# Layer-1 experts: wide and narrow experts alternate block by block, in a TensorE order written in the program, with a gather by rows and a combine in two parts

## The chip, the cores and the metric

The kernel runs on one core of one Trainium2 chip. The metric is the device time of one launch in microseconds (us), as the median of several runs. The core has a matrix engine (PE, with its weight loads shown apart as PEld), a vector engine (DVE), a scalar engine (ACT), a general engine (POOL) and SP, whose queue issues almost all of the DMA transfers. PE writes to PSUM, of which the kernel uses 8 banks of 512 fp32 per partition.

## The reference, cut to what matters

A block of two layers on 256 tokens of width 1024 is followed by a second block of two layers. The change lies in the second layer of the first block, in its mixture of 8 experts with a hidden width of 2816. Each token goes to its two best experts:

```
logits = tokens @ router_w                       # 256 x 8
top_vals, top_idx = top_k(logits, 2);  gates = softmax(top_vals)
for each expert e, over its tokens xb:
    y = (silu(xb @ w1[e]) * (xb @ w3[e])) @ w2[e]
out[token] += gate * y
```

All numbers are fp32. The weights of the 8 experts, 8 x 3 x 1024 x 2816 x 4 bytes = 276.8 MB, are read from HBM once.

## The kernel before

`moe` (line 1171) sorts the experts by their token count. Five places take up to 96 tokens and are called wide here (m = 96, `NL = 5`), three take up to 64 and are called narrow (m = 64). The first place always belongs to expert 0. The rest of the tokens, if any, go through a slow path under `tc.If` (line 1373); no instruction of it shows in the trace.

A `Job` is one expert at its place. Its constructor gathers the expert's tokens: a one-hot matrix `oh` (256 tokens x m slots, in two halves) is multiplied with the tokens, which are kept as a high and a low fp32r part `uh`. Line 1199 uses 128 columns of the tokens as the stationary operand and the one-hot as the moving one, so that the product comes out transposed, features on partitions, in `xg`: 8 groups of features x 4 matmuls with m columns, 32 per job. Two transposes of the one-hot (line 1205) make `oht` for the combine.

The hidden width is cut into blocks of 1024, 1024 and 768. A unit is one block of one job, and consists of three steps:

- `up(i)`: 8 transfers of weights (two of w1 and w3 for each pair of feature groups), then matmuls whose stationary operand is 32 columns of `xg` (wide, four of them side by side on PE) or 64 (narrow, two side by side). A wide job has three such waves for each feature group, in three PSUM banks, a narrow one two, in two banks. ACT then applies silu (line 1236) and DVE multiplies (line 1238), giving `h`.
- `turn(i)`: 8 transposes of `h` (6 for the block of 768) through two banks named hT, copied by ACT and DVE (line 1252).
- `down(i)`: 4 (or 3) transfers of w2, and matmuls that add into the output banks `y` for all three blocks: two banks for a wide job, one for a narrow one. For each 128 of the hidden width there are one and a half waves (wide) or one (narrow).

`combine` (line 1277) brings `y` back to the tokens: for each half of the features it splits `y` into a high and a low part (ACT, DVE), multiplies each with `oht` for both halves of the tokens (line 1296, four matmuls), and DVE adds gate times the product into `acc`, shown as macc (line 1300). For a wide job the second half first needs two copies and a sum (lines 1285 to 1287), because its output lies in parts of two banks.

The loop at line 1332 goes over the units, one expert after another, in the order of `PLACES`: wide, narrow, wide, wide, narrow, wide, wide, narrow. For unit u it calls `up(u)`, then, at the last block, the constructor of the next job, then at the second block the `combine` of the job before, then `down` of the unit before, then `turn(u)`. This is the order of the program; the order on each engine is made by the scheduler of the framework, which may move an instruction that is ready ahead of others. That is how matmuls of a gather or a combine come to stand between those of `up`.

Weights come through `raw` (line 194), which rotates over a ring of SBUF buffers of 1 MB each and issues the transfer on SP's queue as soon as the buffer's last reader is done. The expert's number is loaded into a register on SP (`values_load`, line 1328) ahead of its weights.

The pool of PSUM banks of this stage is set at line 1951: 3 for `up` (tag g), 2 for `y`, 3 (tag b) for all the rest: xg, ohT, hT, comb. Before the stage, PE does a piece of a later layer (`last_v`, shown as lv); after it comes the first layer of the second block, whose first weights are loaded ahead by `prime`.

The later layers' own experts, in `block2`, have a gather of another form (lines 1678 to 1695): the one-hot is the stationary operand and 512 columns of tokens are the moving one, so that rows of tokens come out, in `xs`; eight transposes make `xg` of them.

Of the kernel before, what the change touches and what calls it, by code (L numbers as in the profile page):

```python
# [11 lines left out]
F32 = mybir.dt.float32  # L12
F32R = mybir.dt.float32r
# [9 lines left out]
KC = D // 128  # L23
# [13 lines left out]
CONV = "pvpvpvpp"  # L37
KEX = 4
CAPS = (64,) * KEX + (128,) + (64,) * 5 + (32,) * 6
NL, PLACES = 5, (0, 5, 1, 2, 6, 3, 4, 7)  # L40


def layout(widths):
# [112 lines left out]
class Net:  # L156
# [1014 lines left out]
    def moe(self, E, F, uh, oh0, rank, slot, gates, w1, w3, w2, acc, mp):  # L1171


        nc, tc = self.nc, self.tc
# [3 lines left out]
        def onehot(sl, m, base=0):  # L1178
            oh = mp.tile([128, 2, 96], F32R, tag="oh", name="oh", bufs=2)
            b = base % 128  # L1180
            nc.vector.tensor_tensor(oh[:, :, :m], iotas[base // 128][:, None, b:b + m].to_broadcast([128, 2, m]),
                                    sl[:, :, None].to_broadcast([128, 2, m]), OP.is_equal)
            return oh
# [3 lines left out]
        class Job:  # L1187

            def __init__(j, ws, oh, m, gcol, first):
                j.w = [w.rearrange("(k p) n -> p k n", p=128) for w in ws[:2]]  # L1190
                j.w2, j.m, j.gcol, j.first = ws[2], m, gcol, first
                j.y, j.h, j.hT = None, {}, {}
                j.xg = xg = mp.tile([128, KC, 96], F32, tag="xg", name="xg", bufs=2)
                for k0 in (0, 4):
                    p = self.bank("xg")
                    for i in range(4):
                        o = p[:, i * m:(i + 1) * m]
                        for q in range(4):
                            nc.tensor.matmul(o, uh[q // 2][:, q % 2, (k0 + i) * 128:(k0 + i + 1) * 128], oh[:, q % 2, :m],
                                             start=(q == 0), stop=(q == 3))  # L1200
                    (nc.vector.tensor_copy if k0 else nc.scalar.copy)(xg[:, k0:k0 + 4, :m],
                                                                     p[:, :4 * m].rearrange("p (k t) -> p k t", k=4))
                p = self.bank("ohT")
                for tt in range(2):
                    nc.tensor.transpose(p[:m, tt * 128:(tt + 1) * 128], oh[:, tt, :m].bitcast(F32), self.ident)
                j.oht = mp.tile([128, 256], F32R, tag="oht", name="oht", bufs=2)
                nc.scalar.activation(j.oht[:m], p[:m, :256], AF.Copy)

            def up(j, i):
# [64 lines left out]
                                             start=(i == 0 and k == (k % 2 if b else 0)), stop=(i == len(blocks) - 1 and k >= nk - 2),  # L1274
                                             tile_position=(0, c * t), skip_group_check=True)

            def combine(j):
                m, y = j.m, j.y
                for o in range(2):
                    js = slice(o * 512, (o + 1) * 512)  # L1280
                    src = y[0][:m]
                    if o:
                        if m == 96:
                            src = mp.tile([128, 512], F32, tag="ysum", name="ysum")[:m]
                            nc.scalar.copy(src[:64], y[1][64:128])
                            nc.scalar.copy(src[64:96], y[0][96:128])
                            nc.vector.tensor_tensor(src[:64], y[1][:64], src[:64], OP.add)
                        else:
                            src = y[0][64:128]
                    yg = [self.wkp.tile([128, 512], F32R, tag="room", name="y" + c, bufs=2) for c in "hl"]  # L1290
                    nc.scalar.activation(yg[0][:m], src, AF.Copy)
                    nc.vector.tensor_tensor(yg[1][:m], src, yg[0][:m].bitcast(F32), OP.subtract)
                    for tt in range(2):
                        p = self.bank("comb")
                        for hl in range(2):
                            nc.tensor.matmul(p, j.oht[:m, tt * 128:(tt + 1) * 128], yg[hl][:m], start=(hl == 0), stop=(hl == 1))
                        if j.first:
                            nc.vector.tensor_scalar(acc[:, tt, js], p, j.gcol(tt), None, op0=OP.mult)
                        else:
                            nc.vector.scalar_tensor_tensor(acc[:, tt, js], p, j.gcol(tt), acc[:, tt, js],  # L1300
                                                           op0=OP.mult, op1=OP.add)

        nb = len(blocks)
# [21 lines left out]
        def job(q):  # L1325
            if q == 0:
                return first
            e = nc.values_load(idx[0:1, q:q + 1], engines=(mybir.EngineType.SP,), min_val=0, max_val=E - 1)
            m = 96 if q < NL else 64
            return Job((w1[e], w3[e], w2[e]), onehot(W[:, 0:2, q], m), m, lambda tt: W[:, 2 + tt, q:q + 1], False)  # L1330

        units = [(q, i) for q in PLACES for i in range(nb)]
        jobs = {}
        behind = None
        for u, (q, i) in enumerate(units):
            if u == 0:
                jobs[q] = job(q)
            jobs[q].up(i)
            if i == nb - 1 and u + 1 < len(units):
                q2 = units[u + 1][0]  # L1340
                jobs[q2] = job(q2)
            if i == 1 and behind is not None:
                jobs.pop(behind).combine()
                behind = None
            if u:
                q1, i1 = units[u - 1]
                jobs[q1].down(i1)
                if i1 == nb - 1:
                    behind = q1
            jobs[q].turn(i)  # L1350
        q, i = units[-1]
        jobs[q].down(i)
        jobs.pop(q).combine()


        capv = mp.tile([128, E], F32, name="capv")
# [16 lines left out]
        with self.aside(), tc.If(cnt > self.OV):  # L1373
            rp = mp.tile([128, 2, E], F32, name="rp")
            nc.vector.tensor_tensor(rp, slot, capv[:, None, :].to_broadcast([128, 2, E]), OP.subtract)
            with tc.For_i(0, E, 1) as ei:
                nc.vector.tensor_scalar(ecur, ecur, 1.0, None, op0=OP.add)
                sel = mp.tile([128, E], F32, name="osel")
                nc.vector.tensor_scalar(sel, eid, ecur, None, op0=OP.is_equal)
                pc = mp.tile([128, 2, 2], F32, name="opc")  # L1380
                junk = mp.tile([128, E], F32, name="ojunk")
                for tt in range(2):
                    for i, src in enumerate((rp, G)):
                        nc.vector.scalar_tensor_tensor(junk, src[:, tt, :], 1.0, sel, op0=OP.mult, op1=OP.mult,
                                                       accum_out=pc[:, tt, i:i + 1])
                for b in range(3):
                    j = Job((w1[ei], w3[ei], w2[ei]), onehot(pc[:, :, 0], 64, 64 * b), 64, lambda tt: pc[:, tt, 1:2], False)
                    for i in range(nb):
                        j.up(i)
                        j.turn(i)  # L1390
                        j.down(i)
                    j.combine()
# [509 lines left out]
    def run(self):  # L1902
        nc, t, tc = self.nc, self.t, self.tc
        part = self.part
        with ExitStack() as es:
# [42 lines left out]
                if "l1" in part:  # L1948
                    gpf = self.conv1(mrow)
            e0.close()  # L1950
            self.banks = {"g": 3, "y": 2, "b": 3}
            self.psp = e0.enter_context(tc.tile_pool(name="ps2", bufs=1, space=PSUM))
            if "l1" in part:
                self.moe_layer1(gpf)
# [7 lines left out]
            o = self.out[0].rearrange("(t p) d -> p t d", p=128)  # L1962
# [32 lines left out]
```

## Time and profile before

| what | us |
|---|---|
| median of 3 runs | 2187.96 |
| lowest, highest | 2182.73, 2188.52 |
| the profiled execution | 2188.77 |
| its span, first to last instruction | 2186.9 |
| stage of the layer-1 experts, first `up` to last `down` | 764.6 to 1489.2 |

The trace holds one execution. Times in it count from the first instruction. A row of the timeline is a group of equal instructions: start, length, engine, line, operation, what it writes and reads, partitions x columns, count, and in brackets the engine's idle time before and who ended it. An fp32 matmul of the source shows as two instructions. A matmul's bar holds its latency, and bars of matmuls that run side by side overlap. `128*32 128x512` is a stationary operand of 128 partitions by 32 columns and a moving one of 512 columns. In a window's row the columns behind the busy times are the granted clock of PE as a share of full speed, the mean busy share of the 16 DMA engines, and GB/s.

### The profile page before, as it was taken

Reading aid. Unit: us, or ns where it says so; the run is one execution under the profiler, and the core shown is the slowest. Engines: PE = TensorE matmul, PEld = TensorE weight load, DVE = VectorE, ACT = ScalarE, POOL = GpSimd, SP = SyncE. Lnnn points to the kernel's source line nnn. Section 1 sums busy time; section 2 is a strip of 40 time slices with the busy share of each in tenths; the row PEclk is TensorE's granted clock in tenths of the full one; section 3 lists DMA queues with packets and bytes.
Section 4 is the critical chain, followed back from the end, with each engine's and each line's share of the span. In section 5 each row is a group of like instructions: output and inputs, shape, how many; then the busy total and the mean of one; then the engine's idle time right before and its main releaser. Section 6 shows DMA issues by size and latency. Waiting matters only on the chain. (4 is left out here: it accounts for less than half of the span.)

```text
span 2186.9 us, 32516 instructions
## 1 busy us (share of the span) xinstructions
PE 2022.2 (92%) x13393; PEld 1129.1 (52%) x13393; DVE 827.8 (38%) x1695; ACT 573.6 (26%) x965; POOL 84.4 (4%) x121
## 2 busy tenths in 40 slices
PE   6999897999889899999999999998989987989996
PEld 2777666889867533433344333345733424943331
DVE  4465466444887400111101101015642315662223
ACT  3453345334534300100101001014422212532210
POOL 1010100000120000000000000002000001000000
PEclk9999998999999999999999999998989999999998
DMA  7532547873622689999899998997389999489995
GB/s 289 189 124 93 203 165 274 271 268 116 208 88 99 231 338 374 411 393 361 319 374 402 410 361 315 361 408 278 123 358 386 394 390 365 145 314 404 375 387 245
DMA packets 166338, 634.56 MB, mean 290 GB/s; under 512 B 11952, under 2 KB 53040, under 8 KB 124192
## 3 DMA queue, kind: packets, MB, share of 16 engines
q1 hardware_dynamic: 163808, 630.76, 76.1%
q8 instruction: 111, 1.82, 0.3%
q0 software_dynamic: 2080, 1.04, 0.2%
q10 hardware_dynamic: 288, 0.52, 0.1%
q14 instruction: 51, 0.42, 0.1%
HBM read 631.20 MB, written 1.05 MB: 289 GB/s over the span
## 5 line engine op out<-in xcount | busy, mean ns | idle before, releaser
L1226 PE MATMUL up<-raw,xg 128*32 128x512 f32 (+3 forms) x3456 | 437.6, 559 | 0.1
L256 DVE TENSOR_TENSOR wh<-raw,wh 128x1024 fp32r<-128x1024 f32 x182 | 222.6, 1229 | 178.9 <-ACT wh L255 177.7
L1226 PEld LDWEIGHTS up<-raw,xg 128*32 128x32 f32 (+1 forms) x3456 | 147.4, 114 | 250.8 <-issue 238.4
L255 ACT ACTIVATE wh<-raw 128x1024 fp32r<-128x1024 f32 x182 | 190.7, 1058 | 230.5 <-PE gT L192 88.9
L1272 PE MATMUL y<-raw,hT 128*32 128x512 f32 (+1 forms) x1584 | 218.1, 604 | 0.0
L1728 PE MATMUL up<-raw,xg 128*64 128x512 f32 (+1 forms) x1088 | 205.0, 594 | 4.8 <-DMA raw<-in_w_up 2.9
L1238 DVE TENSOR_TENSOR h<-up,h 64x512 f32<-64x512 f32 (+5 forms) x63 | 40.8, 648 | 389.1 <-ACT h L1236 388.3
L1236 ACT ACTIVATE h<-up 64x512 f32<-64x512 f32 (+5 forms) x63 | 35.0, 555 | 430.7 <-PE up L1226 430.5
L1754 PE MATMUL y<-raw,hT 128*64 128x512 f32 (+1 forms) x576 | 133.2, 597 | 9.0 <-DMA raw<-in_w_down 4.4
L1728 PEld LDWEIGHTS up<-raw,xg 128*64 128x64 f32 (+1 forms) x1088 | 62.8, 127 | 130.9 <-issue 120.9
L1272 PEld LDWEIGHTS y<-raw,hT 128*32 128x32 f32 (+1 forms) x1584 | 60.6, 116 | 123.8 <-issue 116.4
L190 PE MATMUL gT<-fuTh,wh 128*128 128x256 f32 x352 | 101.0, 287 | 0.0
L1734 DVE TENSOR_TENSOR h<-up,h 64x512 f32<-64x512 f32 x28 | 29.6, 1056 | 188.6 <-ACT h L1733 188.6
L191 PE MATMUL gT<-fuTl,wh 128*128 128x256 f32 x352 | 99.5, 283 | 0.0
L192 PE MATMUL gT<-fuTh,wh 128*128 128x256 f32 x352 | 99.5, 283 | 0.0
L445 PE MATMUL mod<-raw,cs 128*32 128x512 f32 x384 | 62.9, 692 | 26.0 <-DMA raw<-in_l_mod_w 26.0
L1754 PEld LDWEIGHTS y<-raw,hT 128*64 128x64 f32 (+1 forms) x576 | 38.4, 124 | 94.0 <-issue 64.7
L1733 ACT ACTIVATE h<-up 64x512 f32<-64x512 f32 x28 | 30.0, 1072 | 188.7 <-PE up L1728 188.7
L190 PEld LDWEIGHTS gT<-fuTh,wh 128*128 128x128 f32 x352 | 67.4, 191 | 12.1 <-issue 10.9
L192 PEld LDWEIGHTS gT<-fuTh,wh 128*128 128x128 f32 x352 | 67.5, 192 | 0.4
L191 PEld LDWEIGHTS gT<-fuTl,wh 128*128 128x128 f32 x352 | 67.4, 192 | 0.2
L1252 DVE COPY hT<-hT 128x384 f32<-128x384 f32 (+3 forms) x24 | 10.8, 449 | 120.7 <-PE hT L1251 120.7
(573 smaller groups left out, 3212.8 us busy)
## 6 DMA issues: line engine op xcount, KB each, us to landing
raw<-in_l_moe_w SPq DMA_DIRECT2D x216, 1024.0 KB, 8.9
raw<-in_w_gate SPq DMA_DIRECT2D x64, 1024.0 KB, 8.9
raw<-in_w_up SPq DMA_DIRECT2D x64, 1024.0 KB, 9.1
raw<-in_w_down SPq DMA_DIRECT2D x64, 1024.0 KB, 11.9
raw<-in_l_mod_w SPq DMA_DIRECT2D x48, 1024.0 KB, 6.2
raw<-in_l_moe_w SPq DMA_DIRECT2D x64, 768.0 KB, 6.4
raw<-in_l_ffn_w SPq DMA_DIRECT2D x33, 1024.0 KB, 5.4
raw<-in_l_w_in SPq DMA_DIRECT2D x14, 1024.0 KB, 5.4
```

The costliest lines, as they stand in the source:

```text
L190: mm(out, l[0], r[0], start=start, stop=False, skip_group_check=True)
L191: mm(out, l[0], r[1], start=False, stop=False, skip_group_check=True)
L192: mm(out, l[1], r[0], start=False, stop=stop, skip_group_check=True)
L255: nc.scalar.activation(hi, x[:, k:k + s, :], AF.Copy)
L256: nc.vector.tensor_tensor(lo, x[:, k:k + s, :], hi.bitcast(F32), OP.subtract)
L445: nc.tensor.matmul(p[32 * j:32 * j + 32, :], self.cs[:, k, :], x[:, 0, j * 512:(j + 1) * 512], start=(k == 0), stop=(k == KC - 1), tile_po ...
L1226: nc.tensor.matmul(ps[b][c * t:(c + 1) * t, :hn], j.xg[:, k, s:s + t], x[w][:, k - k2, half * hn:(half + 1) * hn], start=(k == 0), stop=(k ...
L1236: nc.scalar.activation(h[a:z, js], ps[b1][o1:o1 + z - a, :hn], AF.Silu)
L1238: nc.vector.tensor_tensor(h[a:z, js], ps[b3][o3:o3 + z - a, :hn], h[a:z, js], OP.mult)
L1272: nc.tensor.matmul(j.y[b][c * t:(c + 1) * t, :], hT[:, k, s:s + t], x[:, k - k2, o * 512:(o + 1) * 512], start=(i == 0 and k == (k % 2 if ...
L1728: nc.tensor.matmul(p[o:o + t, :], xg[:, k, c:c + t], pair[w][:, k - k4, :], start=(k == 0), stop=(k == KC - 1), tile_position=(0, o))
L1754: nc.tensor.matmul(y[o][a:a + n, :], hT[:, q * m + a:q * m + a + n], x[e][:, k, o * 512:(o + 1) * 512], start=(q == 0), stop=(q == 3), til ...
```

## The change

The units of wide and narrow experts alternate: the first wide expert's three blocks come first, then blocks are drawn from the row of the other 12 wide ones and from the row of the 9 narrow ones, from whichever has the larger share left. So two jobs are open at a time. The order is (place, block) 0.0 0.1 0.2, 1.0 5.0 1.1 5.1 1.2 5.2 2.0, 2.1 6.0 2.2 6.1 3.0 6.2 3.1, 3.2 7.0 4.0 7.1 4.1 7.2 4.2.

The whole loop stands in `manual_schedule` for PE: PE's instructions keep the order of the program. The other engines are scheduled as before.

The constructor now gathers rows: 8 matmuls with the one-hot as the stationary operand and 512 columns moving, into `xs`, copied by ACT and DVE. The new `begin` transposes these (8 transposes) into `xg` and makes `oht`. The constructor stands ahead of the `up` of the unit before the new job's first, `begin` behind that `up`. `combine` is called for one half of the features between `up` and `down`, and for the other behind `down`, ahead of `turn`.

Three buffers in place of two hold `xg` and `oht`, two of a new tag hold `xs` and `ysum`. PSUM: 3 banks for `y` in place of 2, and 2 in place of 3 for all the rest. The slow path calls `begin` as well.

```diff
-NL, PLACES = 5, (0, 5, 1, 2, 6, 3, 4, 7)
+NL = 5
...
-                j.xg = xg = mp.tile([128, KC, 96], F32, tag="xg", name="xg", bufs=2)
+                j.oh = oh
+                j.xs = xs = [mp.tile([128, 512], F32, tag="half", name="xs", bufs=2) for _ in range(2)]
+                for c in range(2):
+                    cs = slice(c * 512, (c + 1) * 512)
+                    p = self.bank("xs")
+                    for q in range(4):
+                        nc.tensor.matmul(p[:m], oh[:, q % 2, :m], uh[q // 2][:, q % 2, cs], start=(q == 0), stop=(q == 3))
+                    (nc.vector.tensor_copy if c else nc.scalar.copy)(xs[c][:m], p[:m])
+
+            def begin(j):
+                m, xs = j.m, j.xs
+                j.xg = xg = mp.tile([128, KC, 96], F32, tag="xg", name="xg", bufs=3)
                 for k0 in (0, 4):
                     p = self.bank("xg")
                     for i in range(4):
-                        o = p[:, i * m:(i + 1) * m]
-                        for q in range(4):
-                            nc.tensor.matmul(o, uh[q // 2][:, q % 2, (k0 + i) * 128:(k0 + i + 1) * 128], oh[:, q % 2, :m],
-                                             start=(q == 0), stop=(q == 3))
+                        nc.tensor.transpose(p[:, i * m:(i + 1) * m], xs[k0 // 4][:m, i * 128:(i + 1) * 128], self.ident[:m, :m])
...
-            def combine(j):
+            def combine(j, halves=(0, 1)):
                 m, y = j.m, j.y
-                for o in range(2):
+                for o in halves:
...
-        units = [(q, i) for q in PLACES for i in range(nb)]
...
+        streams = [[(q, i) for q in qs for i in range(nb)] for qs in (range(NL), range(NL, E))]
+        units, streams[0] = streams[0][:nb], streams[0][nb:]
+        total = [len(x) for x in streams]
+        while any(streams):
+            units.append(streams[max((0, 1), key=lambda x: len(streams[x]) / total[x])].pop(0))
+        with tc.manual_schedule(engines={mybir.EngineType.PE}):
+            jobs = {units[0][0]: job(units[0][0])}
+            jobs[units[0][0]].begin()
+            done = None
+            for u, (q, i) in enumerate(units):
+                new = u + 1 < len(units) and units[u + 1][1] == 0 and units[u + 1][0]
+                if new:
+                    jobs[new] = job(new)
+                jobs[q].up(i)
+                out, done = done, None
+                if out is not None:
+                    jobs[out].combine((0,))
+                if new:
+                    jobs[new].begin()
+                if u:
+                    q1, i1 = units[u - 1]
+                    jobs[q1].down(i1)
+                    if i1 == nb - 1:
+                        done = q1
+                if out is not None:
+                    jobs.pop(out).combine((1,))
+                jobs[q].turn(i)
+            if done is not None:
+                jobs.pop(done).combine()
+            q, i = units[-1]
+            jobs[q].down(i)
+            jobs.pop(q).combine()
...
-            self.banks = {"g": 3, "y": 2, "b": 3}
+            self.banks = {"g": 3, "y": 3, "b": 2}
```

## Rows read from the trace of the kernel before

**Rows 1.** The page, part 1: busy time of the engines, share, count.

```profile
PE 2022.2 (92%) x13393; PEld 1129.1 (52%) x13393; DVE 827.8 (38%) x1695; ACT 573.6 (26%) x965; POOL 84.4 (4%) x121
```

**Rows 2.** Windows (experts' stage, then three short ones): busy of each engine.

```profile
core 0: us, PE busy (x) PEld busy (x) DVE busy (x) ACT busy (x) POOL busy (x), PEclk, DMA share, GB/s
764.60:1489.20 724.60, 718.23 (x5511) 268.33 (x5510) 90.08 (x148) 65.83 (x126) 0.00 (x0) 0.99 0.96 371
840.00:860.00 20.00, 20.00 (x133) 6.24 (x134) 0.85 (x3) 0.85 (x2) 0.00 (x0) 0.88 0.94 351
1200.00:1220.00 20.00, 18.83 (x124) 6.56 (x124) 1.41 (x3) 1.34 (x3) 0.00 (x0) 0.91 1.02 415
1660.00:1680.00 20.00, 18.39 (x92) 8.65 (x90) 7.95 (x12) 6.00 (x8) 0.00 (x0) 1.00 0.98 385
```

**Rows 3.** Waits of the experts' stage: who waited for whom, us, times, longest.

```profile
PEld up L1226 <- DMA raw<-in_l_moe_w: 2.3, 8, 0.4
...
SPq L200 <- PE up L1226: 363.7, 148, 7.2
SPq L200 <- PE y L1272: 178.7, 78, 9.5
```

**Rows 4.** Groups by line, same stage: count, busy us, mean ns, idle before.

```profile
L1226 PE MATMUL up<-raw,xg 128*32 128x512 f32 (+3 forms) x3456 | 437.6, 559 | 0.1
...
L1272 PE MATMUL y<-raw,hT 128*32 128x512 f32 (+1 forms) x1584 | 218.1, 604 | 0.0
...
L1238 DVE TENSOR_TENSOR h<-up,h 64x512 f32<-64x512 f32 (+5 forms) x63 | 40.8, 648 | 389.1 <-ACT h L1236 388.3
...
L1300 DVE SCALAR_TENSOR_TENSOR macc<-comb,W,macc 128x512 f32<-128x512 f32 x24 | 17.5, 749 | 53.1 <-PE comb L1296 53.1
...
L1252 ACT COPY hT<-hT 128x384 f32<-128x384 f32 (+1 forms) x24 | 10.5, 439 | 119.9 <-PE hT L1251 119.9
```

**Rows 5.** Timeline of PE, two stretches of blocks: start, length, matmuls, count.

```profile
827.70 7.60 PE L1226 MATMUL up<-raw,xg 128*32 128x384 f32 x92
835.23 0.41 PE L1199 MATMUL xg<-oh,muhh 128*128 128x64 f32 x2
...
1211.77 20.83 PE L1226 MATMUL up<-raw,xg 128*32 128x512 f32 x192
1232.53 1.94 PE L1272 MATMUL y<-raw,hT 128*64 128x512 f32 x8
```

**Rows 6.** Timeline of PE: a run of transposes, then runs of a combine.

```profile
867.75 7.93 PE L1272 MATMUL y<-raw,hT 128*32 128x512 f32 x72
875.61 1.09 PE L1251 MATMUL hT<-cst,h 64*128 64x64 f32 x8
876.63 13.95 PE L1226 MATMUL up<-raw,xg 128*64 128x512 f32 x64
...
1064.24 3.63 PE L1226 MATMUL up<-raw,xg 128*32 128x512 f32 x28
1067.80 0.50 PE L1296 MATMUL comb<-yh,oht 96*128 96x512 f32 x1
...
1068.45 2.77 PE L1226 MATMUL up<-raw,xg 128*32 128x512 f32 x20
```

**Rows 7.** Timeline of PE in the later stage: a gather by rows and transposes.

```profile
1674.66 0.63 PE L1685 MATMUL xs<-muhh,oh 128*128 128x512 f32 x2
...
1676.05 0.63 PE L1685 MATMUL xs<-muhl,oh 128*128 128x512 f32 x2
1677.78 1.09 PE L1693 MATMUL xg<-cst,xs 128*128 128x128 f32 x8 [1.11 <-ACT xs L1686]
1678.71 0.38 PE L1703 MATMUL ohT<-cst,oh 128*128 128x128 f32 x2
```

**Rows 8.** Timeline of PE, then DVE: the end of the last expert.

```profile
1476.99 12.24 PE L1272 MATMUL y<-raw,hT 128*64 128x512 f32 x56
...
1494.12 1.41 DVE L1300 SCALAR_TENSOR_TENSOR macc<-comb,W,macc 128x512 f32<-128x512 f32 x2 [0.81 <-PE comb L1296]
```

More of the change, by code (lines that the diff above doesn't have):

```diff
@@ L1204, in __init__ @@
                 for tt in range(2):
-                    nc.tensor.transpose(p[:m, tt * 128:(tt + 1) * 128], oh[:, tt, :m].bitcast(F32), self.ident)
-                j.oht = mp.tile([128, 256], F32R, tag="oht", name="oht", bufs=2)
+                    nc.tensor.transpose(p[:m, tt * 128:(tt + 1) * 128], j.oh[:, tt, :m].bitcast(F32), self.ident)
+                j.oht = mp.tile([128, 256], F32R, tag="oht", name="oht", bufs=3)
                 nc.scalar.activation(j.oht[:m], p[:m, :256], AF.Copy)
@@ L1283, in combine @@
                         if m == 96:
-                            src = mp.tile([128, 512], F32, tag="ysum", name="ysum")[:m]
+                            src = mp.tile([128, 512], F32, tag="half", name="ysum", bufs=2)[:m]
                             nc.scalar.copy(src[:64], y[1][64:128])
@@ L1330, in job @@
             return Job((w1[e], w3[e], w2[e]), onehot(W[:, 0:2, q], m), m, lambda tt: W[:, 2 + tt, q:q + 1], False)
-        units = [(q, i) for q in PLACES for i in range(nb)]
[L1333 to L1353, printed above, removed]
+        streams = [[(q, i) for q in qs for i in range(nb)] for qs in (range(NL), range(NL, E))]
[30 more added lines that the diff above has]
+            jobs.pop(q).combine()
         capv = mp.tile([128, E], F32, name="capv")
@@ L1387, in moe @@
                     j = Job((w1[ei], w3[ei], w2[ei]), onehot(pc[:, :, 0], 64, 64 * b), 64, lambda tt: pc[:, tt, 1:2], False)
+                    j.begin()
                     for i in range(nb):
```

## The prediction

> **What bounds the kernel now.** I read the page's busy times first, then windows over the stage of the layer-1 experts, the waits inside it, its groups by line, and at last the timeline of PE. PE is busy for 92% of the span [rows 1], and in the experts' stage for 718 of 724.6 us [rows 2]; but a matmul's bar contains its latency, so this does not yet say that PE is the limit. DMA's share is 0.96 in the same stage [rows 2], so either could be it. The waits decide: the weight loads of `up` waited for an expert's weights 2.3 us in all, 0.4 us at the longest, while the queue that issues those weights waited for PE's matmuls to give a buffer back 363.7 + 178.7 us, 226 times of 280 issues [rows 3]. Weights are there before PE wants them; PE's own instruction stream is the bound, and the stage is worth what is taken off that stream.
>
> The stream has a floor. A wave of four 32-column matmuls, or of two 64-column ones, takes 0.43 us for 512 columns: 56 narrow matmuls are 28 waves in 12.24 us, of which the last bar is some 0.6 [rows 8]. With 384 columns it is three quarters, 0.32: 92 matmuls, 23 waves, in 7.5 us [rows 5]. Each fp32 matmul of the source is two of the trace, so the 3456 + 1584 of the stage [rows 4] are, by the plans at `up` and `down`, 162 waves at 512 columns and 48 at 384 for each of five wide experts, 108 and 32 for each of three narrow ones, 1134 and 336 together: 487.6 + 108.4 = 596.0 us. The change touches none of them. The other 724.6 - 596.0 = 128.6 us are gathers, transposes of h, combines, waits and clock, put between the waves in 98 runs, of which [rows 6] shows some. That is the pool from which a gain can come.
>
> **The change, part by part.** A run's price is start of the group before it, plus its waves at 0.43, to the start of the group after it. Eight transposes of h: 867.75 + 18 x 0.43 = 875.49, next group 876.63, so 1.14 [rows 6]; I take 1.2, and 1.1 for the six of a 768-wide block. Two combine matmuls: 1064.24 + 7 x 0.43 = 1067.25, next group 1068.45, so 1.2 [rows 6]. Gathering by rows is done by the later stage already: eight 512-column matmuls from 1674.66 to 1676.51, 0.23 each, and eight transposes with two of the one-hot from 1677.78 to about 1678.93, 1.15 together, behind a wait of 1.11 us for the copy between them [rows 7]. From these, for the stage after:
>
> - Turns. 24 units, one run each, since `down` of the unit before stands ahead of it and gives h time: 16 x 1.2 + 8 x 1.1 = 28.0.
> - Gathers. Seven jobs (the first lies before the stage): 56 matmuls at 0.23 = 12.9, standing right behind a turn, so with no run of their own; and 7 x 1.15 = 8.1 for `begin`. The copy's wait of 1.11 is hidden by a whole `up` of at least 10 us put between the two. They replace 224 matmuls and 14 transposes that today stand in scattered runs.
> - Runs of `begin` and of a combine's first half between `up` and `down`: by the order of units there are 11. The fixed part of a run is 1.14 - 8 x 0.11 = 0.26 at a turn and 1.2 - 2 x 0.23 = 0.74 inside `up` [rows 6]; I take the middle, 0.5: 5.5.
> - Combines: 12 halves of four matmuls at 0.23 = 11.2 before the last two jobs, and expert 7's whole combine ahead of the last `down`, 0.3 + 8 x 0.23 + a wait of 1.1 = 3.3.
> - Alternating widths: `up` of a wide block straight into `down` of a narrow one, or the reverse, 11 times without a run between. The row with such a passage shows 1211.77 + 48 x 0.43 = 1232.41 against 1232.53 [rows 5]: 0.12 each, 1.3 in all. The Trainium skill (TensorEngine Tiling, Key Properties) says that changing the tiling mode drains the engine; taken as the fixed part of a whole run, 0.26 to 0.74, that would be 3 to 8 us and not 1.3. The row shows a far smaller drain between two column tilings, and the row goes into the sum.
> - Waits from having two banks for everything but `up` and `y`, where there were three. PE's order is now fixed, so whatever stands behind a bank's copy waits too. The trace of before does not show this arrangement. Lower end: nothing, as the copies are short and off PE. Upper end by the nearest rows, one DVE or ACT operation late each time: 0.3 per gather for the copy of hT (439 ns [rows 4], mostly beside four transposes); 1.0 per `begin`, whose one-hot transposes need a third bank and whose copy queues on ACT behind the silu of h; 0.7 per second half of a combine (macc takes 749 ns [rows 4], twice); 1.5 at the two places where combine and `begin` meet and macc queues on DVE behind three products of h at 648 ns [rows 4]. That is 2.1 + 7.0 + 4.2 + 3.0 = 16.3. I take the whole, being the end that rows support; none excludes twice that.
> - Clock. Two windows show 0.88 and 0.91 [rows 2], that is (0.12 + 0.09) x 20 = 4.2 us lost to half clock. I keep 4.2.
>
> Sum: 596.0 + 28.0 + 12.9 + 8.1 + 5.5 + 11.2 + 3.3 + 1.3 + 16.3 + 4.2 = 686.8, so 37.8 us less. Two things are not free but small: the first job's gather, which now has a copy in its middle but fewer matmuls, 0 +- 0.5; and the end, where a wide expert is last instead of a narrow one. Today the last matmul of `down` ends at 1489.2 and the last macc at 1495.5 [rows 8]; a wide one adds two copies and a sum of about 0.6 each, partly beside the first half: +1.2. Net 36.6.
>
> Is the cover for this still there? DMA is what comes next: 280 transfers, 276.8 MB. At the 415 GB/s of a full window [rows 2] they take 667 us, 20 under PE's 687, and the first buffers of the ring are filled before the stage begins. The register loads for the expert numbers stand on SP ahead of the weights of a unit, once per job, on values ready since before the stage: nothing. The next stage's first four weight loads still follow the last expert's in the same queue.
>
> The profiled execution took 2188.8 us, 0.8 above the median of the three runs; 2188.8 - 36.6 = 2152.2, and on the median's scale **2151 us**. About 0.3% (6.6 us) is what a measurement of this kernel can tell from no change.
>
> **Rivals.**
> First, DMA takes over. Its share is 0.96 [rows 2]; if that were real occupancy, the stage could not get shorter than 0.96 x 724.6 = 696, a gain of 29 - 1 = 28: 2161. Against it: a full window moves 415 GB/s, the stage's mean is 371 [rows 2], and weights wait for buffers. For it: narrow blocks take PE 22 us for 30 us of weights, so stretches of them eat the lead.
>
> Second, nothing gained: if the bank waits are three times my upper end, 49 us, the gain is 36.6 - 32.6 = 4: 2184, inside the 0.3%. For it: a fixed order lets nothing slip past a wait; against it: today's waits of this kind, which the profile puts at a few us, arise with the same copies.
>
> Third, slower, by the clock. In the window from 1200 us PE did narrow waves at 384 columns and a turn, and the clock fell; in the one from 840 us it was still low behind a run of 34 gather matmuls of 64 columns at 835.23 [rows 2, 5]. The change puts eight more transposes into each job and sets them in runs with the one-hot's, the combine's halves and h's. If every one of the 36 runs after let the clock fall once, at the 0.12 x 20 = 2.4 us that the window from 840 us lost, against the 4.2 us in the sum, it would cost 36 x 2.4 - 4.2 = 82 us: 2233. It decides against the change from 15 such falls on beyond today's (36.6 / 2.4). Against it: the later stage runs the same matmuls and transposes with a wait of 1.1 us in the middle, and its window has a clock of 1.00 [rows 7, 2]. The Trainium skill (TensorE: Matmul & The Clock Gate, Part 4: PE-mode transpose) says that transposes do not count as busy work for the clock, which is the rule that speaks against gathering by transposes. By that rule this rival is right; the window of the later stage does not bear it out for groups of ten between dense matmuls.
>
> **How the numbers follow.** Forecast, waits from none to twice the upper end: the gain runs from 36.6 + 16.3 + 4.2 = 57 down to 36.6 - 16.3 = 20, 2131 to 2168, chance 0.64. DMA: 0.12 (faster too). Waits between two and three times, 2168 to 2181: 0.06. Nothing gained: 0.08. Slower: 0.10, of which the clock has 0.06. So faster 0.82, same 0.08, slower 0.10; the range from 2130 to 2180 leaves out the last two and little else.
>
> **What would show it.** Right: waves unchanged in number and pace; runs of other matmuls down from 98 to about 36; no more gather matmuls with 64 or 96 columns; PE's stage near 687 us; DMA's rate in it near 390 GB/s; waits of `up` for weights still a few us. Wrong step by step: waits of transposes or one-hot transposes for DVE or ACT above 16 us in all (banks); waits of `up` for weights above 10 us (DMA); more than two windows with a clock under 0.95 (clock). A stage time above 718 us would make the forecast wrong.

## The result, and the profile after

| what | before | after |
|---|---|---|
| median (runs taken side by side) | 2186.15 us, 4 runs, 2182.73 to 2188.52 | 2157.77 us, 4 runs, 2149.66 to 2160.15 |
| ratio, 95% interval | | 0.9855, 0.9837 to 0.9873 |
| the profiled execution | 2188.77 us | 2155.77 us |
| its span | 2186.9 us | 2153.9 us |

The change makes the kernel 1.45% faster. The forecast was 2151 us, in a range from 2130 to 2180. Placed on the two profiled executions, the time went here:

| stretch | before | after | difference | forecast |
|---|---|---|---|---|
| start to first `up` | 764.6 | 761.9 | -2.7 | 0 +- 0.5 |
| layer-1 experts' stage | 724.6 | 688.9 | -35.7 | -37.8 |
| last `down` to the end | 697.7 | 703.0 | +5.3 | +1.2 |
| span | 2186.9 | 2153.9 | -33.0 | -36.6 |

The busy times on the page after answer to [rows 1]:

```profile
PE 1982.9 (92%) x13265; PEld 1102.5 (51%) x13265; DVE 831.4 (39%) x1703; ACT 577.9 (27%) x973; POOL 82.9 (4%) x121
```

PE's share has not moved, though the span is 33 us shorter, so the share alone could not have told this change from none. The next rows are windows of the kernel after, columns as in [rows 2]: the whole stage, the later stages, and four windows of the stage with a low clock.

```profile
761.90:1450.80 688.90, 675.35 (x5399) 239.57 (x5398) 93.43 (x155) 68.94 (x132) 0.00 (x0) 0.99 0.98 391
1450.80:2153.80 703.00, 614.15 (x3230) 323.49 (x3226) 291.74 (x593) 190.08 (x284) 28.25 (x38) 0.94 0.80 316
780.00:800.00 20.00, 17.53 (x152) 5.64 (x148) 2.63 (x4) 2.25 (x4) 0.00 (x0) 0.91 0.71 258
1060.00:1080.00 20.00, 17.80 (x150) 5.68 (x143) 4.89 (x8) 3.11 (x6) 0.00 (x0) 0.91 1.03 412
1260.00:1280.00 20.00, 17.52 (x125) 6.84 (x123) 5.97 (x10) 1.82 (x4) 0.00 (x0) 0.91 1.02 413
1430.00:1450.00 20.00, 18.04 (x102) 6.21 (x102) 5.37 (x9) 1.66 (x3) 0.00 (x0) 0.83 0.58 216
```

In the stage DMA moved 391 GB/s instead of 371 (in both kernels 13 of the 280 weight transfers had been issued ahead of the first `up`), and two windows with a low clock have become four. Are weights late now? These are the stage's waits after, as in [rows 3], with PE's two longest ones for another engine:

```profile
PE xg L1208 <- DVE macc L1308: 4.1, 4, 2.0
...
PEld up L1234 <- DMA raw<-in_l_moe_w: 3.9, 14, 0.4
PEld y L1280 <- DMA raw<-in_l_moe_w: 3.8, 11, 0.6
...
PE hT L1259 <- DVE h L1246: 2.5, 1, 2.5
```

They are not: 7.7 us in 25 waits, none over 0.6. PE still sets the pace. The groups by line answer to [rows 4]:

```profile
L1234 PE MATMUL up<-raw,xg 128*32 128x512 f32 (+3 forms) x3456 | 403.6, 560 | 0.0
L1280 PE MATMUL y<-raw,hT 128*32 128x512 f32 (+1 forms) x1584 | 208.6, 608 | 0.0
...
L1246 DVE TENSOR_TENSOR h<-up,h 64x512 f32<-64x512 f32 (+5 forms) x63 | 40.8, 647 | 390.3 <-ACT h L1244 389.5
```

The counts, 3456 and 1584, and the duration of one are nearly as before; the busy time of `up` fell from 437.6 to 403.6. This fits fewer interruptions by runs of other matmuls, each of which shows a bar's latency once: with 62 runs fewer, as counted next, it is 0.55 us for each, and a bar takes 0.56. Counted in the order of PE's matmuls, the runs of others between the waves went from 97 to 35 (forecast about 36; the prediction's 98 counted one more), and their price, worked out as in the prediction (so with what the waves just ahead of a run lost to a low clock), from 129.3 to 91.2 us.

Where the four low windows come from is seen in PE's timeline after (columns as in [rows 5]; in brackets the idle time before and who ended it):

```profile
779.50 3.19 PE L1234 MATMUL up<-raw,xg 128*32 128x512 f32 x28
785.16 1.10 PE L1259 MATMUL hT<-cst,h 96*128 96x96 f32 x8 [2.47 <-DVE h L1246]
...
1066.79 0.39 PE L1304 MATMUL comb<-yl,oht 64*128 64x512 f32 x1
1069.19 0.46 PE L1208 MATMUL xg<-cst,xs 64*128 64x64 f32 x4 [2.00 <-DVE macc L1308]
1069.85 0.64 PE L1208 MATMUL xg<-cst,xs 64*128 64x64 f32 x4 [0.20 <-DVE macc L1308]
1070.42 0.63 PE L1213 MATMUL ohT<-cst,oh 128*64 128x128 f32 x2
1070.99 11.66 PE L1280 MATMUL y<-raw,hT 128*32 128x512 f32 x96
...
1433.97 1.05 PE L1259 MATMUL hT<-cst,h 96*128 96x96 f32 x6
1435.36 0.50 PE L1304 MATMUL comb<-yh,oht 64*128 64x512 f32 x1 [0.35 <-ACT hT L1260]
...
1437.61 0.47 PE L1304 MATMUL comb<-yh,oht 64*128 64x512 f32 x1 [0.47 <-ACT yh L1299]
1438.90 0.79 PE L1304 MATMUL comb<-yl,oht 64*128 64x512 f32 x1 [0.82 <-DVE yl L1300]
...
1440.48 10.35 PE L1280 MATMUL y<-raw,hT 128*32 128x512 f32 x72
```

Three kinds of places. The first turn has no `down` ahead of it, so PE waits 2.47 us for `h`; that run costs 3.70. At the two joint places (the first half of one expert's combine, then `begin` of the next) PE waits for macc, 2.00 at the first and 1.72 at the second, and 0.20 more at each; they cost 5.12 and 4.45. The last turn has expert 7's whole combine behind it: 6.82. PE's clock drops to its lower level, 1.2 of 2.4 GHz, at 786.6, 1069.9, 1264.5 and 1438.6 us, for 17.1 us together (summed from the trace's record of the granted clock; 10.2 before). Why macc is late shows on DVE:

```profile
1066.25 2.10 DVE L1246 TENSOR_TENSOR h<-up,h 64x512 f32<-64x512 f32 x3 [20.21 <-ACT h L1244]
1068.39 1.41 DVE L1308 SCALAR_TENSOR_TENSOR macc<-comb,W,macc 128x512 f32<-128x512 f32 x2
```

The three products of `h` stand ahead of it on DVE's queue, and PE's next matmul, in its fixed order, needs the bank that macc empties.

### The profile page after: what moved, and what is told of

It is laid out like the page before. It is cut to its first block, busy times and chain, and to the rows that moved or that the text cites. A ratio compares the mean times of both kernels' runs of the same rounds, so it can differ in the third digit from the quotient of the medians.

```text
span 2153.9 us, 32324 instructions
## 1 busy us (share of the span) xinstructions
PE 1982.9 (92%) x13265; PEld 1102.5 (51%) x13265; DVE 831.4 (39%) x1703; ACT 577.9 (27%) x973; POOL 82.9 (4%) x121
## 3 DMA queue, kind: packets, MB, share of 16 engines
q1 hardware_dynamic: 163808, 630.76, 76.2%
## 5 line engine op out<-in xcount | busy, mean ns | idle before, releaser
L1234 PE MATMUL up<-raw,xg 128*32 128x512 f32 (+3 forms) x3456 | 403.6, 560 | 0.0
L1234 PEld LDWEIGHTS up<-raw,xg 128*32 128x32 f32 (+1 forms) x3456 | 133.0, 115 | 255.0 <-issue 248.5
L1280 PE MATMUL y<-raw,hT 128*32 128x512 f32 (+1 forms) x1584 | 208.6, 608 | 0.0
L192 PEld LDWEIGHTS gT<-fuTh,wh 128*128 128x128 f32 x352 | 67.5, 192 | 0.4
L1260 ACT COPY hT<-hT 128x384 f32<-128x384 f32 (+1 forms) x24 | 10.5, 438 | 165.2 <-PE hT L1259 142.5
```

What stands on the lines that cost most here:

```text
L192: mm(out, l[1], r[0], start=False, stop=stop, skip_group_check=True)
L1234: nc.tensor.matmul(ps[b][c * t:(c + 1) * t, :hn], j.xg[:, k, s:s + t], x[w][:, k - k2, half * hn:(half + 1) * hn], start=(k == 0), stop=(k ...
L1280: nc.tensor.matmul(j.y[b][c * t:(c + 1) * t, :], hT[:, k, s:s + t], x[:, k - k2, o * 512:(o + 1) * 512], start=(i == 0 and k == (k % 2 if ...
```

## Experiments: which part brings the gain

The theory: the gain lies in fewer and shorter interruptions of PE's stream, above all through the fixed order; alternating widths only rearranges units whose weights were never late. The rivals: alternation brings it, or the form of the gather does. Four kernels were compared side by side.

**One expert after another, all else kept** (`e_seq`):

```diff
-        streams = [[...
+        units = [(q, i) for q in (0, 5, 1, 2, 6, 3, 4, 7) for i in range(nb)]
...
-                    jobs[out].combine((0,))
+                    jobs.pop(out).combine()
...
-                if out is not None:
-                    jobs.pop(out).combine((1,))
...
-            self.banks = {"g": 3, "y": 3, "b": 2}
+            self.banks = {"g": 3, "y": 2, "b": 3}
```

> The changed kernel's fixed TensorE order and gather by rows, but one expert after another in the places of before (0 5 1 2 6 3 4 7), each combine whole between up and down, and the banks of before (2 for y, 3 for the rest). Theory (the gain lies in fewer and cheaper runs between the waves; alternation only rearranges the units): stage 685 to 700 us against 689.0 with the change and 724.6 before, waits of up for weights below 10 us, 2150 to 2170 us in all. Rival (alternation brings the gain, as it evens out what DMA must deliver): the weight waits rise above 15 us, stage 705 or more, 2175 or more.

**The scheduler's order** (`e_free`):

```diff
-        with tc.manual_schedule(engines={mybir.EngineType.PE}):
+        if True:
```

> The changed kernel with the fixed TensorE order taken away: the scheduler may again move matmuls between the waves. Theory: the runs between waves come back, 70 or more against 35, and at some 0.5 us of fixed cost each the stage is 15 to 30 us longer than 689.0: 704 to 719, 2173 to 2188 in all. Rival (gather by rows or alternation brings the gain, the order does not): stage within 6 us of 689.0, 2151 to 2164.

**Before, with the gather by rows alone** (`e_rows`): the constructor of before with the eight matmuls and the eight transposes of the diff in place of its 32 matmuls.

> The kernel of before with the gather by rows and transposes alone; order of units, scheduler, banks as before. Theory: the matmuls that remain still stand in scattered runs; eight matmuls of 0.23 and eight transposes of 0.11 replace 32 of 0.11, about 1 us less per expert, and the gather's runs fall from some 45 to some 25 at 0.5 us of fixed cost each: 10 to 17 us less than before's 724.6, so 707 to 715, 2170 to 2178 in all. Rival 1 (the gather is the whole gain): stage below 695, 2160 or less. Rival 2 (the clock: transposes let it fall): no gain, or more stretches at half clock than before's two.

**After, with the old gather** (`e_oldgather`): the 32 matmuls stand in `begin`, in place of its eight transposes; `xs` is gone.

> The changed kernel with the old gather: 32 matmuls per expert straight into the transposed form, all placed where the transposes of begin stand now, in the fixed order. Theory: 32 x 0.11 to 0.12 in place of 8 x 0.23 and 8 x 0.11 is 0.7 to 1.1 us more per expert, 5 to 8 us over seven: stage 694 to 697, 2163 to 2166 in all. Rival 1 (the form of the gather matters most): stage 705 or more. Rival 2 (the clock falls because of the transposes): fewer than the four stretches at half clock, and stage 689 or less.

| kernel | units | order on PE | gather | runs | their price | stage | median | ratio to before |
|---|---|---|---|---|---|---|---|---|
| before | one by one | scheduler | columns | 97 | 129.3 | 724.6 | 2187.13 | |
| `e_rows` | one by one | scheduler | rows | 100 | 118.2 | 715.3 | 2179.03 | 0.9961 (0.9945 to 0.9977) |
| `e_free` | alternating | scheduler | rows | 83 | 110.0 | 705.5 | 2167.82 | 0.9917 (0.9891 to 0.9943) |
| `e_seq` | one by one | fixed | rows | 38 | 98.1 | 693.4 | 2157.27 | 0.9872 (0.9846 to 0.9898) |
| `e_oldgather` | alternating | fixed | columns | 35 | 96.0 | 693.3 | 2164.15 | 0.9905 (0.9878 to 0.9933) |
| after, first profile | alternating | fixed | rows | 35 | 91.2 | 688.9 | | |

The windows of the stages of the four kernels, one fence each in the order of the table, the last with two windows at its joint places:

```profile
766.00:1481.30 715.30, 708.93 (x5399) 251.29 (x5398) 94.93 (x155) 69.99 (x133) 0.00 (x0) 1.00 0.97 376
```

```profile
763.80:1469.30 705.50, 698.32 (x5399) 254.15 (x5398) 94.69 (x155) 69.37 (x132) 0.00 (x0) 1.00 0.97 382
```

```profile
762.90:1456.30 693.40, 673.50 (x5399) 239.18 (x5398) 94.05 (x155) 69.78 (x133) 0.00 (x0) 0.99 0.97 386
```

```profile
766.00:1459.30 693.30, 683.11 (x5511) 255.56 (x5510) 88.64 (x148) 65.29 (x125) 0.00 (x0) 0.98 0.98 389
1060.00:1080.00 20.00, 18.00 (x122) 9.56 (x118) 4.89 (x8) 3.12 (x6) 0.00 (x0) 0.78 1.03 410
1260.00:1280.00 20.00, 18.30 (x146) 9.37 (x142) 4.20 (x7) 2.80 (x6) 0.00 (x0) 0.83 1.02 409
```

The path from before to after through `e_rows` and `e_seq` reads: gather by rows 9.3 us, fixed order 21.9, alternation with its split combine and banks 4.5. The middle step holds more than the order: `e_seq` also parts `begin` from the constructor and has a third buffer for `xg`. The order alone is taken away in `e_free`, where with alternating units it is worth 705.5 - 688.9 = 16.6 (13.6 against a second execution of the kernel after, 691.9, below). So the fixed order is the largest part either way. The rival that alternation evens out DMA falls: with one expert after another the weights' waits were 3.7 us at `up` and 5.4 at `down`, against 3.9 and 3.8. The little that alternation brings lies, as far as the runs' prices show, in the combines, which stand whole between `up` and `down` in `e_seq`; PE's timeline there shows one:

```profile
888.28 0.40 PE L1304 MATMUL comb<-yl,oht 96*128 96x512 f32 x1
889.22 0.50 PE L1304 MATMUL comb<-yh,oht 96*128 96x512 f32 x1 [0.54 <-ACT yh L1299]
891.16 0.50 PE L1304 MATMUL comb<-yl,oht 96*128 96x512 f32 x1 [1.44 <-DVE yl L1300]
```

The second half waits 0.54 + 1.44 us for its parts, and seven such runs cost 4.71 to 6.29 each; a half of a combine that stands alone costs 1.26 in the kernel after.

The theory was wrong on a point of `e_rows`. It expected the gather's runs to fall to some 25; there are still 100 runs in all, because the scheduler put single matmuls of the gather between waves, 28 of them at 0.75 us each. Its stage and its median are both just past the slow edge of what was expected. And the gather itself is worth less in a fixed order, 693.3 - 688.9 = 4.4 us, or 1.4 against that second execution, by which alternation too would be worth 1.5 and not 4.5: these two are small, and known no closer than that. In the time of the whole kernel alternation does not show: the ratio of `e_seq` lies within the noise of the 0.9855 of the kernel after. `e_oldgather`'s stage came 0.7 us under what was expected. It had three stretches at half clock in place of four, as its second rival wanted, but longer ones, 23.9 us in all, and its stage was not under 689. `e_free` had its stage in the expected range but a median 5 us under it, because the later stages took 695.4 us there and not the 703 that the expectation had taken over (below).

## Experiments: the three places that cost more than the rest

Do these places really cost what their runs show, or does the wait only move on? Each was taken away alone, then all together.

**No joint places** (`e_nojoint`): expert 7 begins one unit earlier, expert 5 is combined one unit later.

```diff
+                new = 7 if u == 16 else new if u != 17 else False
...
-                out, done = done, None
+                out = None
+                if not (u == 10 and done == 5):
+                    out, done = done, None
```

> The changed kernel without the two places where a combine's first half and a begin meet between up and down: expert 7 is begun one unit earlier, expert 5 combined one unit later. Theory: two runs of 5.12 and 4.45 us become four of 1.6, 1.3, 1.6, 1.3, so 3.8 us less, and the two half-clock stretches of 3.4 us (1.7 us lost each, partly inside those runs) go: stage 684 to 686 us. Rival (the waits only move to another place): 688 to 690, with runs above 4 us at the new places.

**Expert 7's combine between the waves of the last `down`** (`e_end`): `down` takes calls to make ahead of a given pair of hidden groups.

```diff
-            if done is not None:
-                jobs.pop(done).combine()
...
-            jobs[q].down(i)
+            jobs[q].down(i, {2: lambda: jobs[done].combine((0,)), 4: lambda: jobs[done].combine((1,))})
```

> The changed kernel with expert 7's combine laid between the waves of the last down, one half at a time, in place of a run with the last turn ahead of that down. Theory: the run of 6.82 us becomes 1.2 + 1.3 + 1.3 = 3.8, and the half-clock stretch of 6.8 us behind it shortens: stage 685 to 687 us (3 less), the rest unchanged. Rival (expert 7's macc now delays expert 4's at the end): the saving is lost again behind the last matmul of down, 6.0 us today, 9 then.

**Job 1's rows ahead of the first turn** (`e_first`): the constructor of job 1 stands behind the first `up`, its `begin` behind the second.

```diff
+                if u == 0:
+                    jobs[1] = job(1)
...
-                if new:
+                if u == 1 or (new and new != 1):
```

> The changed kernel with the rows of job 1 gathered between the first up and the first turn, and its begin behind the second up, the rest as changed. Theory: the first turn's run stays 3.7 to 3.9 us, but the run that held those eight matmuls before falls from 3.6 to 5.1 down to 1.2 to 1.7 us, and the half-clock stretch behind the first turn goes: stage 685 to 688 us. Rival (the register load for job 1 on SP delays the weights behind it): waits of up or down for weights above 10 us, stage 689 or more.

**All three** (`e_all`), and the kernel after once more beside it (`e_again`):

> Three edits together: no joint places, expert 7's combine between the waves of the last down, and job 1's rows gathered between the first up and the first turn, where TensorE waits 2.5 us for h. Theory: 3.8 + 3.0 + 2.3 us of runs and some 2 to 4 us of clock: stage 676 to 681 us, 2144 to 2152 in all. Rival (DMA is next: at 391 GB/s it was at 0.98 of its share): the saved time returns as waits for weights, stage 685 or more, weight waits above 12 us against 7.7.

> The changed kernel once more, to see what repeats. Theory (the runs of the layer-1 experts set their stage; the stage behind it varies by its clock from execution to execution): stage 688 to 690 us again, its half-clock stretches again at the first turn, the two joint places and the end, while the time of the later stage, 702.2 us against 696.8 before, moves by some us. Rival (the change itself makes the later stage longer, through what it leaves in the weight ring or the banks): later stage 701 to 703 us again.

| kernel | runs | their price | half clock in the stage | stage |
|---|---|---|---|---|
| after, first and second profile | 35, 35 | 91.2, 94.0 | 17.1, 23.9 | 688.9, 691.9 |
| `e_nojoint` | 37 | 85.5 | 13.7 | 682.9 |
| `e_end` | 37 | 89.3 | 13.7 | 684.6 |
| `e_first` | 35 | 85.9 | 10.2 | 683.3 |
| `e_all` | 39 | 77.5 | 0 | 672.8 |

The stages of the four edited kernels came out 0.4 to 3.2 us under what was expected; that of `e_again`, expected at 688 to 690, came out 1.9 over it, with its low clock at the same four places but for 23.9 us. Against the first profile the three edits gave 6.0, 4.3 and 5.6 us, 15.9 together; the kernel with all three gave 16.1. Against the second it would be 9.0, 7.3 and 8.6, 24.9 together and 19.1, so these sums hold no closer than the 3 us between the two profiles. That the waits did not move on is seen in PE's idle time in the stage, the window less PE's busy time. It was 13.6 us in the first profile after (688.90 - 675.35) and 13.4 in the second, though their low clock differed; it is 9.7, 11.6 and 11.3 with one edit each, and 6.2 with all three. The windows of the stage with one edit, in the order of the table:

```profile
768.40:1451.30 682.90, 673.23 (x5399) 239.20 (x5398) 93.68 (x155) 69.02 (x132) 0.00 (x0) 0.99 0.99 395
763.30:1447.90 684.60, 673.05 (x5399) 239.09 (x5398) 93.40 (x155) 69.01 (x132) 0.00 (x0) 0.99 0.99 394
766.80:1450.10 683.30, 672.02 (x5399) 239.07 (x5398) 93.42 (x155) 69.02 (x132) 0.00 (x0) 0.99 0.99 395
```

The whole kernel took 2155.95, 2145.44 and 2148.88 us in the one run of each single edit. That is no gain for `e_nojoint`, whose first `up` came 7 us later than in the kernel after; the stages tell more here than the whole. `e_all`'s windows, the stage and then the stretches that held the four places:

```profile
768.40:1441.20 672.80, 666.65 (x5399) 237.75 (x5398) 93.44 (x155) 69.01 (x132) 0.00 (x0) 1.00 1.01 400
...
780.00:800.00 20.00, 19.54 (x172) 7.06 (x168) 3.32 (x5) 2.84 (x5) 0.00 (x0) 1.00 0.81 315
1060.00:1080.00 20.00, 19.79 (x190) 6.19 (x182) 2.79 (x5) 2.53 (x5) 0.00 (x0) 1.00 1.03 409
1260.00:1280.00 20.00, 19.44 (x140) 7.73 (x138) 6.23 (x10) 1.95 (x4) 0.00 (x0) 1.00 1.02 414
1420.00:1440.00 20.00, 19.66 (x154) 7.20 (x150) 6.22 (x10) 3.12 (x6) 0.00 (x0) 1.00 0.97 376
```

PE was busy for 17.5 to 18.0 of 20 us at those places after, and is for 19.4 to 19.8 now, at full clock. The first turn, a passage from a wide `up` to a narrow `down`, and a piece of the last `down` in `e_all`'s timeline of PE:

```profile
790.57 0.62 PE L1199 MATMUL xs<-muhl,oh 128*96 128x512 f32 x2
791.65 1.31 PE L1259 MATMUL hT<-cst,h 96*128 96x96 f32 x8 [0.46 <-DVE h L1246]
...
915.09 20.81 PE L1234 MATMUL up<-raw,xg 128*32 128x512 f32 x192
935.83 7.09 PE L1282 MATMUL y<-raw,hT 128*64 128x512 f32 x32
...
1430.80 2.78 PE L1282 MATMUL y<-raw,hT 128*32 128x512 f32 x24 [0.34 <-ACT hT L1260]
1433.51 0.49 PE L1306 MATMUL comb<-yh,oht 64*128 64x512 f32 x1
...
1434.63 2.78 PE L1282 MATMUL y<-raw,hT 128*32 128x512 f32 x24
```

The gather of job 1 fills the wait for `h` (0.46 left of 2.47), and a half of the combine laid between waves meets no wait at all. The median of `e_all` was 2140.25 us (2136.88 to 2143.37) beside 2156.58 of the kernel after (2153.9 to 2158.38) and 2190.31 of before: ratio 0.9767 (0.9746 to 0.9788), against 0.984 (0.982 to 0.986) of the kernel after. It beats both. The rival, DMA as the next bound, did not show: at 400 GB/s the weights' waits of `up` were 2.0 us.

The clock goes with it. In `e_first` the first drop is gone with the wait, in `e_nojoint` the two at the joint places, in `e_end` the one at the end, in `e_all` all. It is no exact rule: `e_first` had no drop at its second joint place either, though PE waited 1.72 there as before, so its 5.6 us are not all the edit's; `e_nojoint` had a new drop, of 3.4 us at 1114.3, behind half a combine and a turn with a wait of 0.38, a run that `e_all` has too and without a drop; and the first turn of `e_end`, with its wait of 2.5 us, had none in the first execution and one in the second.

## Experiments: what the later stages gave back

After the last `down`, the kernel after took 5.3 us more than before, in code whose PE instructions come in the same order. Two kernels of the last series, and `e_seq` of the first, were run again for this.

> The kernel with expert 7's combine between the waves of the last down once more, now timed. What is tested is the stage behind the layer-1 experts, whose TensorE instructions are the same in every kernel here and which took 695.7 us in this kernel's first execution, 703.1 and 703.2 in the changed kernel's. Theory A (the time of that stage varies with its half-clock stretches from execution to execution, whatever the kernel): it lies elsewhere now, 698 to 703, with its half-clock stretches at 0.38 us per us above the line of the other runs; the median of the runs is 2150 to 2155. Theory B (each kernel fixes it, through when its stage begins): 695 to 697 again, 63 us at half clock, median 2144 to 2148.

> The kernel with one expert after another once more. Experts' stage 692 to 695 us as before. Theory A (the stage behind varies from execution to execution): another value than 695.8, up to 703. Theory B (each kernel fixes it): 695 to 697 again, with 63 us at half clock.

> The kernel with the three edits together once more: experts' stage 671 to 675 us again without a stretch at half clock in it; the stage behind at 671.3 + 0.385 x its time at half clock, as in the other runs (700.4 us at 76.5 us in the first execution), so 695 to 703. The rival, that the half clock inside the stage had only by chance stayed away: two stretches or more, stage 676 or more.

| kernel | half clock behind the last `down` | time behind it |
|---|---|---|
| before | 67.5 | 697.7 |
| after, twice | 82.5, 82.4 | 703.0, 703.2 |
| `e_end`, twice | 63.1, 63.0 | 695.7, 695.6 |
| `e_seq`, twice | 62.8, 63.3 | 695.7, 696.2 |
| `e_all`, twice | 76.4, 76.2 | 700.4, 699.9 |
| `e_first` | 70.0 | 696.9 |
| `e_free`, `e_rows` | 63.2, 72.8 | 695.4, 698.6 |
| `e_oldgather`, `e_nojoint` | 78.8, 79.3 | 702.4, 702.9 |

The record of the clock ends some 2 us behind the last instruction, at half clock in every run; the column holds these 2 us too.

The windows behind the last `down`, of the kernel after (second profile), then of `e_end` (second):

```profile
1453.40:2156.60 703.20, 613.79 (x3230) 324.05 (x3226) 292.63 (x593) 190.12 (x284) 27.33 (x38) 0.94 0.80 316
```

```profile
1449.80:2145.40 695.60, 606.92 (x3226) 318.49 (x3226) 292.58 (x593) 190.12 (x284) 29.13 (x38) 0.96 0.81 320
```

The same matmuls take 613.8 us of PE against 606.9, at a clock of 0.94 against 0.96. Over the table the time follows the half clock, (703.2 - 695.6) / (82.4 - 63.0) = 0.39 us for each us. I had taken it for chance between executions (theory A); theory B held: each of four kernels repeated its value within 0.5 us in its two profiled executions, though the first `up` moved by up to 2.6 us between the two. So the 5.3 us belong to the kernel after as built, and are no effect of the alternation, since `e_end` alternates too and has the least. `e_end2`'s median, 2146.73 us (2144.91 to 2150.53; ratio 0.981, 0.9792 to 0.9828), fits: its gain of some 10 us on the kernel after is 5 to 8 in the stage and 7 behind it, less a first `up` that came some 4 us later. What sets the drops for a kernel was not found; it stays open. `e_all2` repeated the stage at 672.9 without a drop in it.

## Why the prediction was right, and where its sizes were off

- **PE as the bound, waves untouched**: right. 688.9 - 91.2 = 597.7 us lie outside the runs, against 596.0 in the sum. (A slip in the sum: its 12 halves of four matmuls at 0.23 are 11.0, not 11.2.)
- **The stage**: 686.8 forecast, 688.9 and 691.9 measured; runs 36 against 35; DMA 390 against 391 GB/s; waits for weights "a few us" against 7.7.
- **The terms inside**: several errors cancel. Five `begin` that stand alone cost 1.59 each; the sum had 1.15 + 0.5 + 1.0 = 2.65, mainly as the one-hot transposes wait 0.24 for ACT and not 1.0 (5.3 us too much). A turn with a gather behind it costs 3.52 to 3.72 (a fifth 5.10, with the low clock of the waves ahead of it), against 1.1 or 1.2 + 1.84 + 0.3 = 3.2 or 3.3: with "no run of their own" the gathers are nearly as cheap as forecast (2 us too little, beside that clock). The last run, 1.1 + 3.3 in the sum, cost 6.82 (2.4 too little). The first turn was counted at the price of the others, with "24 units, one run each, since `down` of the unit before stands ahead of it"; the first unit has none, and cost 3.70 (2.5 too little).
- **Bank waits**: 16.3 forecast; PE's own rows of waits for copies, macc and the parts of y sum to about 11 us, 4.1 of them at the joint places. Most of the difference is the 1.0 per `begin` named above.
- **Mode changes**: 0.12 each forecast. The row of `e_all` where a wide `up` passes into a narrow `down` gives 915.09 + 48 x 0.43 = 935.73 against 935.83, so 0.10. The Trainium skill (TensorEngine Tiling, Key Properties) says that a change of the tiling mode drains the engine; the measurement agrees at most with a drain of 0.1 us, not with the price of a whole run.
- **Clock**: the step that failed by size. "I keep 4.2" rested on two low windows; there were four, which by the prediction's own measure lost (3 x 0.09 + 0.17) x 20 = 8.8 us. At half clock PE spent 17.1 and 23.9 us in the two profiles against 10.2 before (5.1 us lost, of which the two windows had caught 4.2), and another 15 us behind the stage. At 0.39 us each the latter is 5.9, enough for the 5.3 that the later stages gave back, where the prediction had only its +1.2 for a wide last expert. That end was in fact no longer: last matmul of `down` to last macc 6.0 us, against 6.3. By the prediction's own test, more than two windows under 0.95, this step was wrong.
- **Start**: the 2.7 us gained ahead of the first `up` are about the 2.6 us by which this point moved between two executions of one kernel, and well within the 9 us between all executions.
- **The rivals**: DMA did not take over, not even at 400 GB/s; its bound of 696 us was passed by 688.9 and by 672.8. Nothing gained: the waits are no more than the upper end. Slower by the clock: the mechanism was there, at four places of 35 and not in each run. `e_oldgather` shows that transposes were not what decided: with 32 plain matmuls in place of the gather's eight the drops at the joint places were no shorter (10.2 and 6.8 us, against 3.4 twice and 6.8 twice in the two profiles after), and `e_all`, with all the transposes, had none. The Trainium skill (TensorE: Matmul & The Clock Gate, Part 4: PE-mode transpose) says that a transpose does not count as busy work in the same way; the traces here neither refute that nor need it: of seven `begin` of ten transposes in `e_all`, none had a drop behind it.

## What to carry to other kernels

When one engine's instruction stream is the bound, count the interruptions of its long runs and what each costs, and take the order into your own hands: here the order alone was worth 14 to 17 us of 36, and 22 with the gather's pieces set apart, more than the new gather or the new order of units. In a fixed order nothing slips past a wait (PE's idle time in the stage is 13.6 us, against 7.2 with the scheduler's order in `e_free`), so look then for the few places with nothing to do ahead of a wait (the first unit, the last one, two small steps that share a bank), and put independent matmuls there; three such edits gave another 16 to 19 us. Compare kernels stage by stage: stages that a change does not touch differed by 7 us here, in step with the clock.

## What the runs showed that was not expected

- The half clock of untouched stages repeated per kernel (63 us in two executions of one, 82.5 in two of another), while the start of the stage moved by up to 2.6 us between two executions of one kernel.
- Runs of about the same price differed in what the clock did. Of ten joint runs of 4.45 to 5.17 us, in which PE waited 1.7 or 2.0 us, nine saw it drop, and the second one of `e_first` did not; nor did runs of 4.97 and 5.07 us in `e_all`, where no wait of PE was over 0.4 us. In `e_seq`, twice, it dropped at each of the combines with a wait of 2.21 to 2.45 us and at none of those with 1.44.
- In `e_rows` a scheduler that is free to move matmuls made 28 separate interruptions of 28 gather matmuls, at 0.75 us each, where 0.23 is the pace of one that stands in a row of eight.
